# The last pooling layer multiplies before it takes its means, and state updates keep their traced place

## The chip, the cores and the metric

The kernel runs on one core of a Trainium2 chip. The metric is the device time of one execution in microseconds (us). The names are those of the profile: PE is the matrix engine (TensorE) and PEld its weight loads, DVE is VectorE, ACT is ScalarE, POOL is GpSimd, SP is the queue that issues most of the DMAs.

## The reference

One inference step of a four-layer decoder: 256 new prompt tokens and 8 sample tokens of width 1024, 264 columns in all. Each layer has a token mixer (pooling, gated delta rule, retention, pooling again) and then a dense feed-forward block (FFN), and each sublayer ends in a LayerNorm. Cut to what matters here:

```python
def pool_mixer(x, buf, n_valid, w, scale):            # four channel groups, windows 2, 4, 8, 16
    ext = concatenate([buf, x], axis=1)               # buf: the last 15 rows of the state
    c = pad(cumsum(ext, axis=1))
    for gi, win in enumerate(POOL_WINDOWS):
        s = c[:, P+1:P+1+T, lo:hi] - c[:, P+1-win:P+1-win+T, lo:hi]
        means.append(s / minimum(t + 1 + n_valid, win))
    pooled = concatenate(means, -1) - x
    return einsum('btgc,gcd->btgd', pooled, w) * scale, ext[:, -P:]

S = S * gl_n[..., None, None] + einsum('bhcd,bhce->bhde', kg_n, v_new)   # delta rule and retention alike

x = layer_norm(DN_ALPHA * x + mix, ln_g[i, 0], ln_b[i, 0])
x = layer_norm(DN_ALPHA * x + swiglu(x, ffn_w13[i], ffn_w2[i]), ln_g[i, 1], ln_b[i, 1])
```

The mean over tokens and the product with `w` over channels act on different axes, so either can come first.

## The kernel before

The activations lie transposed: 8 blocks of 128 channels, each 264 tokens wide. Every float32 operand is split into a rounded high part and a low rest, and `mm3` (L123 holds its matmuls) makes each product of three matmuls: high times high, low times high, high times low. Weights come in chunks of 1 MB into three `raw` buffers by SP; ACT casts the high part (L205), DVE takes the low part (L206), in `split`.

A norm can be **deferred** (class `LN`): the centred sum `d` times its gain goes into `zh` and `zl`, the next layer multiplies these at once, and only then do `stats` (L344) give the scale `r` and the shift `mr`. `unfold` (L397) repairs a product: one DVE instruction from the PSUM bank times `r`, one POOL addition. `apply` (L387) makes `x` itself: one DVE instruction, one POOL addition, and the split of `x` into `xh` and `xl`. A norm that is not deferred waits for `stats`, and `finish` (L376) makes `x`. Deferred are all norms but those after FFN 2 and FFN 3.

Each **FFN** (`ffn`, L444) has three stages on PE. In the first, steps j = 0 to 7 multiply `zh` and `zl`, and each step unfolds two products, gates them (`evac`) and applies one block of `x` (the *z stage* below). Steps 8 to 21 multiply `xh` and `xl` (the *x stage*). Then `w2` multiplies the gated `gh` and `gl` (the *g stage*). FFN 1 follows the delta rule and FFN 2 the retention layer; each also updates the 8 sample tokens' states of all 8 heads, in `gdn_states` (L413) and `ret_states` (L428). The program asks for four updates after every step from j = 8 on and after every second chunk of the g stage (`next(more, None)`), which ends in the g stage. An update is a multiplication on ACT (L421, L437) and one on DVE (L422, L438); a head's state and its new row come through two buffers each (SP loads `st` and `vbc`), and POOL stores the state.

A planner orders the instructions of every engine ahead of the run, by an estimate of when each is ready. Updates depend on little, so they can be placed far ahead of where the program asks for them. `tc.keep_in_program_order` ties an instruction behind the one that was traced before it on its engine; what is traced later can still pass it.

The **last pooling layer** (`pool_layer`, L497) follows FFN 2, whose norm is not deferred. It takes the window sums of `x` (L551, for window 16 on POOL), splits the means into `ph` and `pl` (L558, L559), multiplies them with its matrix, adds `ALPHA * x` (L568), and its own deferred norm makes `zh` and `zl` for FFN 3. Matmuls on a tile of ones (`busy`) fill PE's time meanwhile. The tile `d` has one buffer (L279), `zh` and `zl` share two (L286, L287).

Of the kernel before, what the change touches and what calls it, by code (L numbers as in the profile page):

```python
# [11 lines left out]
F32 = mybir.dt.float32  # L12
F32R = mybir.dt.float32r
# [98 lines left out]
def body(ctx: ExitStack, tc: tile.TileContext, ap):  # L112
# [75 lines left out]
    def nm(s):  # L188
        uid[0] += 1
        return f"{s}_{uid[0]}"  # L190

    def mm_ps(spare=False):
        if spare:
            return sm_ps([P, T + 2])
        return pmm.tile([P, T + 2], F32, tag="mm", name=nm("mm"))

    def sm_ps(shape):
        return psm.tile(shape, F32, tag="sm", name=nm("sm"))
# [70 lines left out]
    class LN:  # L269
# [3 lines left out]

        def __init__(self, idx, defer, on_pe=False):
            self.idx, self.defer, self.on_pe = idx, defer, on_pe
            self.c, self.seen = None, []
            self.d = pers.tile([P, KB, T], F32, tag="d", name=nm("d"))  # L279
            if on_pe:  # L280
                self.p1, self.p2 = sm_ps([P, T]), sm_ps([P, T])
            else:
                self.s1 = lnp.tile([P, T], F32, tag="s1", name=nm("s1"))
                self.s2 = lnp.tile([P, T], F32, tag="s2", name=nm("s2"))
            if defer:
                self.zh = pers.tile([P, KB, T + 2], F32R, tag="xz", name=nm("zh"), bufs=2)  # L286
                self.zl = pers.tile([P, KB, T + 2], F32R, tag="xz", name=nm("zl"), bufs=2)  # L287
                G.tensor_copy(self.zh[:, :, T:T + 2], gbh[:, idx])
                G.tensor_copy(self.zl[:, :, T:T + 2], gbl[:, idx])

# [93 lines left out]
                V.scalar_tensor_tensor(y, self.d[:, m], gm, self.r, MUL, MUL)  # L384
                S.activation(x[:, m], y, AF.Identity, bias=bm)  # L385

        def apply(self, m):  # L387

            u = lnp.tile([P, T], F32, tag="u", name=nm("u"), bufs=2)
            S.activation(u, self.mr, AF.Identity, scale=self.ng[:, m:m + 1], bias=W("lnb", self.idx * 8 + m))  # L390
            y = lnp.tile([P, T], F32, tag="y", name=nm("y"), bufs=2)
            V.scalar_tensor_tensor(y, self.d[:, m], self.g(m), self.r, MUL, MUL)
            G.tensor_tensor(x[:, m], y, u, ADD)
            S.copy(xh[:, m], x[:, m])  # L394
            V.tensor_tensor(xl[:, m], x[:, m], xh[:, m].bitcast(F32), SUB)  # L395

# [9 lines left out]
    def resid(ln, m, ps):  # L406
# [3 lines left out]
            V.tensor_tensor(ln.d[:, m], ps, ln.d[:, m], ADD)  # L410
        ln.block(m)

    def gdn_states(fp):  # L413

        for h in range(H):
            st = fp.tile([P, NB, P], F32, tag="st", name=nm("st"), bufs=2)
            vbc = fp.tile([P, NB, P], F32, tag="vbc", name=nm("vbc"), bufs=2)
            nc.sync.dma_start(st, ap["gst"][h])
            nc.sync.dma_start(vbc, vdg[h].rearrange("b e -> (b e)").partition_broadcast(P).rearrange("p (b e) -> p b e", b=NB))
            for b in range(NB):  # L420
                S.mul(st[:, b], st[:, b], egs[:, b, h:h + 1])  # L421
                V.scalar_tensor_tensor(st[:, b], vbc[:, b], ksg[:, h, b:b + 1], st[:, b], MUL, ADD)  # L422
                if b % 4 == 3:
                    if b > 4:
                        nc.gpsimd.dma_start(ap["gdn_s"][h], st)
                    yield

    def ret_states(fp):  # L428

        for h in range(H):  # L430
            st = fp.tile([P, NB, 256], F32, tag="st", name=nm("st"), bufs=2)
            vbc = fp.tile([P, NB, 256], F32, tag="vbc", name=nm("vbc"), bufs=2)
            nc.sync.dma_start(st, ap["rst"][h])
            nc.sync.dma_start(vbc, vdr[h].rearrange("b e -> (b e)").partition_broadcast(P).rearrange("p (b e) -> p b e", b=NB))
            for b in range(NB):
                if b % 2 == 0:
                    S.mul(st[:, b:b + 2], st[:, b:b + 2], 1.0 - 2.0 ** (-5.0 - h))  # L437
                V.scalar_tensor_tensor(st[:, b], vbc[:, b], ksr[:, h, b:b + 1], st[:, b], MUL, ADD)  # L438
                if b % 4 == 3:
                    if b > 4:  # L440
                        nc.gpsimd.dma_start(ap["ret_s"][h], st)
                    yield

    def ffn(l, pln):  # L444
        with tc.tile_pool(name=f"ffn{l}", bufs=1) as fp:
            gh = fp.tile([P, FB, T], F32R, name=nm("gh"))
            gl = fp.tile([P, FB, T], F32R, name=nm("gl"))

            more = (gdn_states if l == 1 else ret_states)(fp) if l in (1, 2) else iter(())

            def evac(j, pa, pb):
                s = fp.tile([P, T], F32, tag="s", name=nm("s"), bufs=2)
                S.activation(s, pa, AF.Silu)
                V.tensor_tensor(s, s, pb, MUL)
                S.copy(gh[:, j], s)
                V.tensor_tensor(gl[:, j], s, gh[:, j].bitcast(F32), SUB)

            for j in range(FB):
                if j < ND:
                    pss = proj2(ap["w13"][l, j], pln.zh, pln.zl, j == 2)  # L460
                    if j == 0:
                        pln.stats()
                    ab = [fp.tile([P, T], F32, tag="ab", name=nm("ab"), bufs=4) for _ in range(2)]
                    for e in range(2):
                        pln.unfold(pss[e], ab[e])
                    evac(j, *ab)
                    for m in range(KB * j // ND, KB * (j + 1) // ND):
                        pln.apply(m)
                else:
                    pa, pb = proj2(ap["w13"][l, j], xh, xl)  # L470
                    evac(j, pa[:, 0:T], pb[:, 0:T])
                    next(more, None)
            ln = LN(l * 2 + 1, l in (0, 1))
            tc.keep_in_program_order(S.preload_act_table_set("natural_log_exp_and_others"))
            hl = None
            ps = None
            for t in range(KB * FB):
                m, k = divmod(t, FB)
                if t % 16 == 0:
                    hl = chunk(ap["w2"][l, t // 16])  # L480
                if k == 0:
                    ps = mm_ps()
                mm3(ps[:, 0:T], hl[(t % 16) // 8], (t % 8) * 128, 128, gh[:, k], gl[:, k], k == 0, k == FB - 1)
                if k == FB - 1:
                    resid(ln, m, ps[:, 0:T])
                if t % 16 == 8:
                    next(more, None)
            assert next(more, None) is None
            if not ln.defer:
                ln.stats()  # L490
                for m in range(KB):
                    ln.finish(m)
                    if l == DEPTH - 1 and m % 2:
                        nc.sync.dma_start(ap["y"][:, m - 1:m + 1], x[:, m - 1:m + 1])
            return ln

    def pool_layer(l, j, _):  # L497
        with tc.tile_pool(name=f"pool{l}", bufs=1) as pp:
            st = pp.tile([P, KB, NB, 15], F32, name=nm("st"))
            ob = pp.tile([P, 512], BF16, name=nm("ob"))  # L500
# [900 lines left out]
```

## Time and profile before

| | us |
|---|---|
| median of 3 runs (lowest, highest) | 1423.22 (1420.69, 1425.02) |
| the profiled execution's own time | 1423.15 |
| its span, first to last instruction | 1421.4 |
| PE, DVE, ACT, POOL busy | 1335.9, 1043.1, 847.0, 458.4 |

Busy times are means over stages with different limits. The way to read this profile is to cut the span at the points where PE goes over from one kind of operand to the next (the first matmul on `zh`, on `xh`, on `gh`), and to compare like stages of the four FFNs, which do the same products.

### The profile page before, as it was taken

The numbers are of one execution on the slowest core, as the hardware profiler recorded it, in microseconds if no ns is written. First come the engines' busy times: TensorE is split into PE (matmuls) and PEld (weight loads), VectorE is DVE, ScalarE is ACT, GpSimd is POOL, SyncE is SP. The second block draws the span as 40 slices with busy tenths as digits, with TensorE's granted clock in tenths as the row PEclk, the third lists the DMA queues.
The fourth block names the chain that finished last, engine by engine and source line by source line (L and its number), as shares of the span: only waits on it lengthen the run. The fifth ranks groups of instructions, "written<-read, shape, count | busy, mean of one in ns | idle before, by whom it ended". The sixth has DMA issues, their size and how long they took to land. (4 is left out here: it accounts for less than half of the span.)

```text
span 1421.4 us, 27703 instructions
## 1 busy us (share of the span) xinstructions
PE 1335.9 (94%) x10506; PEld 1280.3 (90%) x10509; DVE 1043.1 (73%) x2075; ACT 847.0 (60%) x1975; POOL 458.4 (32%) x518
## 2 busy tenths in 40 slices
PE   7999999879999988999979999999899998999996
PEld 4999999768998987999979999998899995999996
DVE  8885566998666898656687867669987648885564
ACT  4674544759555688544476655547866444774543
POOL 5230013554352434001267755132400135330022
PEclk8999999899999999999999999999999998999998
DMA  6355555412222578555544644359798452355551
GB/s 226 119 181 179 178 179 199 148 60 90 90 96 79 206 285 280 178 179 177 195 179 153 224 171 177 140 178 362 280 394 311 176 180 89 119 189 181 179 183 42
DMA packets 44341, 257.06 MB, mean 181 GB/s; under 512 B 5040, under 2 KB 9776, under 8 KB 16560
## 3 DMA queue, kind: packets, MB, share of 16 engines
q1 hardware_dynamic: 35936, 223.17, 44.2%
q10 hardware_dynamic: 5968, 19.55, 3.8%
q0 software_dynamic: 2304, 12.58, 2.2%
q8 instruction: 82, 1.34, 0.4%
q14 instruction: 51, 0.42, 0.1%
HBM read 238.45 MB, written 16.84 MB: 180 GB/s over the span
## 5 line engine op out<-in xcount | busy, mean ns | idle before, releaser
L206 DVE TENSOR_TENSOR l<-raw,h 128x512 fp32r<-128x512 f32 x658 | 461.6, 737 | 149.9 <-ACT h L205 144.5
L205 ACT CAST h<-raw 128x512 fp32r<-128x512 f32 x680 | 386.9, 617 | 226.7 <-PE mm L123 180.1
L123 PE MATMUL mm<-xh,h 128*128 128x264 f32 x1216 | 346.5, 288 | 8.8 <-ACT xh L394 5.2
L123 PE MATMUL mm<-xl,h 128*128 128x264 f32 x1216 | 348.4, 288 | 6.0 <-DVE xl L395 6.0
L123 PE MATMUL mm<-xh,l 128*128 128x264 f32 x1216 | 343.8, 287 | 0.4 <-DVE l L206 0.4
L123 PEld LDWEIGHTS mm<-xh,h 128*128 128x128 f32 x1216 | 229.9, 190 | 11.4 <-ACT xh L394 6.3
L123 PEld LDWEIGHTS mm<-xl,h 128*128 128x128 f32 x1216 | 231.0, 190 | 7.0 <-DVE xl L395 6.6
L123 PEld LDWEIGHTS mm<-xh,l 128*128 128x128 f32 x1216 | 229.0, 190 | 1.0 <-DVE l L206 0.6
L123 PE MATMUL mm<-gh,l 128*128 128x264 f32 x704 | 200.7, 285 | 0.0
L123 PE MATMUL mm<-gh,h 128*128 128x264 f32 x704 | 200.3, 285 | 0.0
L123 PE MATMUL mm<-gl,h 128*128 128x264 f32 x704 | 198.7, 282 | 0.0
L123 PE MATMUL mm<-zh,h 128*128 128x266 f32 x496 | 144.7, 296 | 9.1 <-DVE ab L403 8.5
L123 PE MATMUL mm<-zh,l 128*128 128x266 f32 x496 | 143.3, 294 | 6.2 <-DVE l L206 6.2
L123 PE MATMUL mm<-zl,h 128*128 128x266 f32 x496 | 145.1, 294 | 0.0
L123 PEld LDWEIGHTS mm<-gh,h 128*128 128x128 f32 x704 | 132.5, 188 | 0.1
L123 PEld LDWEIGHTS mm<-gh,l 128*128 128x128 f32 x704 | 132.5, 188 | 0.1
L123 PEld LDWEIGHTS mm<-gl,h 128*128 128x128 f32 x704 | 132.6, 188 | 0.0
L313 POOL TENSOR_TENSOR s<-d 128x264 f32<-128x264 f32 x6 | 5.7, 942 | 361.7 <-DVE d L297 361.7
L123 PE MATMUL mm<-xh,w 128*128 128x264 f32 x416 | 108.8, 316 | 2.1 <-DVE ab L403 2.1
L123 PEld LDWEIGHTS mm<-zh,h 128*128 128x128 f32 x496 | 95.7, 194 | 11.2 <-ACT h L205 5.3
L123 PEld LDWEIGHTS mm<-zh,l 128*128 128x128 f32 x496 | 95.5, 194 | 8.1 <-DVE l L206 7.7
L404 POOL TENSOR_TENSOR ab<-ab,u 128x264 f32<-128x264 f32 x68 | 64.9, 963 | 116.3 <-PE mm L123 39.3
(403 smaller groups left out, 2792.8 us busy)
## 6 DMA issues: line engine op xcount, KB each, us to landing
raw<-in_w_dram SPq DMA_DIRECT2D x132, 1024.0 KB
raw<-in_rwi_dram SPq DMA_DIRECT2D x24, 1024.0 KB
raw<-in_gwi_dram SPq DMA_DIRECT2D x16, 1024.0 KB
st<-in_rst_dram ACTq DMA_DIRECT2D x8, 1024.0 KB
raw<-in_rwo_dram SPq DMA_DIRECT2D x8, 1024.0 KB
st<-in_rst_dram SPq DMA_DIRECT2D x8, 1024.0 KB
vbc<-vdr SPq DMA_DIRECT2D x8, 1024.0 KB
out_ret_s_dram<-st POOLq DMA_DIRECT2D x8, 1024.0 KB, 10.5
```

What stands on the lines that cost most here:

```text
L123: i = nc.tensor.matmul(*a, **k)
L205: S.copy(hi[:, w], src_ap[:, w])
L206: (E or V).tensor_tensor(lo[:, w], src_ap[:, w], hi[:, w].bitcast(F32), SUB)
L313: G.tensor_tensor(self.s1, d[:, self.seen[0]], d[:, m], ADD)
L404: (E or G).tensor_tensor(out, out, u[:n], ADD)
```

## The change

Two things are changed. First, each of the four kinds of state-update instruction is tied behind the instruction traced before it on its engine. Second, the norm after FFN 2 is deferred, and the last pooling layer is a new function: `pool_rows` (called at the start of FFN 2's g stage) loads the state rows and sums them into eight more columns of `zh` and `zl`; `pool_late` multiplies `zh`, `zl` with the matrix, takes `stats`, unfolds the products, and takes the window sums of these. `x` is made by `apply` without its split. The state of the last pooling layer is stored by POOL from a `raw` buffer.

```diff
-        return pmm.tile([P, T + 2], F32, tag="mm", name=nm("mm"))
+        return pmm.tile([P, n], F32, tag="mm", name=nm("mm"))
...
-                self.zh = pers.tile([P, KB, T + 2], F32R, tag="xz", name=nm("zh"), bufs=2)
-                self.zl = pers.tile([P, KB, T + 2], F32R, tag="xz", name=nm("zl"), bufs=2)
+                self.zh = pers.tile([P, KB, T + 2 + more], F32R, tag="xz", name=nm("zh"), bufs=2)
+                self.zl = pers.tile([P, KB, T + 2 + more], F32R, tag="xz", name=nm("zl"), bufs=2)
...
             G.tensor_tensor(x[:, m], y, u, ADD)
+            if not parts:
+                return
...
+    def later(i):
+        return tc.keep_in_program_order(i)
...
-                S.mul(st[:, b], st[:, b], egs[:, b, h:h + 1])
-                V.scalar_tensor_tensor(st[:, b], vbc[:, b], ksg[:, h, b:b + 1], st[:, b], MUL, ADD)
+                later(S.mul(st[:, b], st[:, b], egs[:, b, h:h + 1]))
+                later(V.scalar_tensor_tensor(st[:, b], vbc[:, b], ksg[:, h, b:b + 1], st[:, b], MUL, ADD))
...
-                    S.mul(st[:, b:b + 2], st[:, b:b + 2], 1.0 - 2.0 ** (-5.0 - h))
-                V.scalar_tensor_tensor(st[:, b], vbc[:, b], ksr[:, h, b:b + 1], st[:, b], MUL, ADD)
+                    later(S.mul(st[:, b:b + 2], st[:, b:b + 2], 1.0 - 2.0 ** (-5.0 - h)))
+                later(V.scalar_tensor_tensor(st[:, b], vbc[:, b], ksr[:, h, b:b + 1], st[:, b], MUL, ADD))
...
-            ln = LN(l * 2 + 1, l in (0, 1))
+            ln = LN(l * 2 + 1, l < DEPTH - 1, more=NB if l == 2 else 0)
+            if l == 2:
+                pool_rows(ln)
...
+    def pool_rows(ln):
+
+        st = wp.tile([P, CW], F32, tag="raw", name=nm("raw"))[:, 0:KB * NB * 15].rearrange("p (k b r) -> p k b r", k=KB, b=NB)
+        nc.sync.dma_start(st, ap["pst"][1])
+        nc.gpsimd.dma_start(ap["pool_o"][1], st)
+        ss = lnp.tile([P, KB, NB], F32, tag="ss", name=nm("ss"))
+        for g in range(4):
+            w = slice(2 * g, 2 * g + 2)
+            V.tensor_reduce(ss[:, w], st[:, w, :, 16 - (2 << g):15], AX.X, ADD)
+        zh, zl = (z[:, :, T + 2:T + 2 + NB] for z in (ln.zh, ln.zl))
+        S.copy(zh, ss)
+        V.tensor_tensor(zl, ss, zh.bitcast(F32), SUB)
+
+    def pool_late(l, j, pln):
...
+            raw = wp.tile([P, CW], F32, tag="raw", name=nm("raw"))
+            nc.sync.dma_start(raw, ap["pw"][j])
+            hl = [split(raw[:, i * 1024:(i + 1) * 1024], 1024, wp, "w", G) for i in range(2)]
...
+            def product(g):
+                for e in range(2):
+                    ps = pss[2 * g + e] = mm_ps(n=T + 2 + NB)
+                    for kk in range(2):
+                        mm3(ps, hl[g // 2], (g % 2) * 512 + kk * 256 + e * 128, 128, pln.zh[:, 2 * g + kk], pln.zl[:, 2 * g + kk], kk == 0, kk == 1)
+
+            product(0)
+            product(1)
+            pln.stats()
+            ln = LN(l * 2, True, True)
+            pob = sm_ps([P, 512])
+            busy(8)
+            for g in range(4):
+                b0 = 2 * g
+                win = 2 << g
+                E = G if g == 3 else V
+                y = pp.tile([P, 2, T], F32, tag="y", name=nm("y"), bufs=2)
+                rows = []
+                for e in range(2):
+                    ps = pss[b0 + e]
+                    pln.unfold(ps, y[:, e])
+                    rows.append(ps[:, T + 2:T + 2 + NB])
+                dst = pp.tile([P, 2, T], F32, tag="s0", name=nm("sw"), bufs=2)
+                if g == 0:
...
+                else:
+                    src = y
+                    for i in range(g + 1):
+                        sh = 1 << i
+                        if i:
+                            dst = pp.tile([P, 2, T], F32, tag=f"s{i % 2}", name=nm("sw"), bufs=2)
+                        E.tensor_tensor(dst[:, :, sh:TP], src[:, :, sh:TP], src[:, :, 0:TP - sh], ADD)
+                        S.copy(dst[:, :, 0:sh], src[:, :, 0:sh])
+                        src = dst
+                    for e in range(2):
+                        V.tensor_tensor(dst[:, e, TP:T], rows[e], y[:, e, TP:T], ADD)
+                    V.tensor_tensor(dst[:, :, 0:16], dst[:, :, 0:16], co[:, b0:b0 + 2], MUL)
+                    V.scalar_tensor_tensor(dst, dst, 1.0 / win, y, MUL, SUB)
+                if g < 2:
+                    product(g + 2)
+                for m in (b0, b0 + 1):
+                    pln.apply(m, False)
+                S.mul(ax[:, b0:b0 + 2], x[:, b0:b0 + 2], ALPHA)
+                if g:
+                    G.tensor_tensor(ax[:, b0:b0 + 2], ax[:, b0:b0 + 2], ln.c.unsqueeze(1).to_broadcast([P, 2, T]), SUB)
+                for e in range(2):
+                    m = b0 + e
+                    V.scalar_tensor_tensor(ln.d[:, m], dst[:, e], W("psc", j * 8 + m) if g else hps[:, e:e + 1], ax[:, m], MUL, ADD)
+                    if g:
+                        ln.centre(m, False)
+                if g == 0:
+                    ln.estimate(b0, b0 + 1)
+                if g < 3:
+                    busy(8)
...
```

## Rows read from the trace of the kernel before

**Rows 1.** The page's first part: busy us, share of the span, instructions

```profile
PE 1335.9 (94%) x10506; PEld 1280.3 (90%) x10509; DVE 1043.1 (73%) x2075; ACT 847.0 (60%) x1975; POOL 458.4 (32%) x518
```

**Rows 2.** Instructions on zh: count, ns min/median/max, first to last start, FFN 3

```profile
L123 PE MATMUL mm<-zh,h x112: 280/286/482, 1207.5 to 1257.9; 128*128 128x266 f32 x112
```

**Rows 3.** Busy time by stage: z of FFN 0, then z and x of FFN 1, 2, 3

```profile
core 0: us, PE busy (x) PEld busy (x) DVE busy (x) ACT busy (x) POOL busy (x), PEclk, DMA share, GB/s
35.70:87.00 51.30, 51.18 (x405) 50.59 (x404) 43.33 (x79) 37.34 (x91) 16.93 (x19) 1.00 0.38 127
...
486.90:549.70 62.80, 54.18 (x390) 51.50 (x389) 60.02 (x135) 51.33 (x139) 26.55 (x31) 0.95 0.80 288
549.70:641.40 91.70, 86.41 (x673) 84.99 (x674) 58.01 (x113) 52.93 (x119) 8.41 (x11) 0.96 0.57 194
963.00:1023.70 60.70, 52.91 (x390) 51.56 (x389) 57.33 (x114) 48.85 (x113) 18.78 (x23) 0.94 0.86 328
1023.70:1106.80 83.10, 82.67 (x675) 82.34 (x674) 65.62 (x128) 53.98 (x111) 10.00 (x12) 1.00 0.89 343
1207.50:1258.30 50.80, 50.80 (x405) 50.32 (x404) 43.64 (x79) 37.55 (x91) 17.26 (x19) 1.00 0.37 128
1258.30:1342.30 84.00, 82.99 (x674) 82.44 (x674) 52.17 (x94) 44.86 (x97) 5.12 (x6) 1.00 0.53 187
```

**Rows 4.** The state updates: count, ns min/median/max, first to last start

```profile
L421 ACT ACTIVATE st<-st,egs x64: 384/387/417, 490.9 to 564.7; 128x128 f32<-128x128 f32 x64
L422 DVE SCALAR_TENSOR_TENSOR st<-vbc,ksg,st x64: 338/341/849, 497.0 to 565.1; 128x128 f32<-128x128 f32 x64
L437 ACT ACTIVATE st<-st x32: 612/620/635, 968.1 to 1090.0; 128x512 f32<-128x512 f32 x32
L438 DVE SCALAR_TENSOR_TENSOR st<-vbc,ksr,st x64: 472/480/980, 971.8 to 1092.2; 128x256 f32<-128x256 f32 x64
```

**Rows 5.** Retention states: waits at FFN 2's start, stores to landing, a stretch's DMA rate

```profile
968.14 2.19 ACT L437 ACTIVATE st<-st 128x512 f32<-128x512 f32 x4 [0.91 <-DMA st<-in_rst_dram]
...
971.79 1.67 DVE L438 SCALAR_TENSOR_TENSOR st<-vbc,ksr,st 128x256 f32<-128x256 f32 x4 [2.72 <-DMA vbc<-vdr]
...
out_ret_s_dram<-st POOLq DMA_DIRECT2D x8, 1024.0 KB, 10.5
...
1035.00:1040.00 5.00, 5.00 (x44) 5.00 (x43) 4.42 (x9) 3.77 (x10) 0.00 (x0) 1.00 1.01 426
```

**Rows 6.** DVE and ACT in order of time around the last pooling layer: start, us

```profile
1171.41 0.43 DVE L410 TENSOR_TENSOR d<-mm,d 128x264 f32<-128x264 f32 x1 [6.56 <-PE mm L123]
...
1179.04 0.43 DVE L368 SCALAR_TENSOR_TENSOR r<-t,r 128x264 f32<-128x264 f32 x1
...
1205.82 0.64 ACT L558 ACTIVATE ph<-sw 128x528 fp32r<-128x528 f32 x1 [1.02 <-DVE sw L557]
...
1210.14 1.11 DVE L568 SCALAR_TENSOR_TENSOR d<-mm,vec,ax 128x264 f32<-128x264 f32 x2 [2.95 <-PE mm L123]
```

**Rows 7.** Busy time by stage, columns as above: from the norm's r to FFN 3

```profile
1179.50:1207.50 28.00, 22.94 (x97) 15.38 (x97) 25.43 (x40) 15.80 (x40) 14.18 (x13) 0.82 0.13 43
```

**Rows 8.** DVE and POOL in order of time, alone and beside each other

```profile
525.59 0.42 DVE L403 TENSOR_TENSOR ab<-mm,r 128x264 f32<-128x264 f32 x1
...
1182.79 0.48 DVE L384 SCALAR_TENSOR_TENSOR y<-d,vec,r 128x264 f32<-128x264 f32 x1
...
1188.95 0.69 DVE L557 SCALAR_TENSOR_TENSOR sw<-sw,x 128x528 f32<-128x528 f32 x1
...
1191.56 1.80 DVE L557 SCALAR_TENSOR_TENSOR sw<-sw,x 128x528 f32<-128x528 f32 x1
...
1189.71 4.81 POOL L562 TENSOR_TENSOR ax<-ax,c 128x528 f32<-128x528 f32 x3 [1.72 <-ACT c L331]
```

**Rows 9.** The additions of unfold and apply on POOL: count, ns min/median/max

```profile
L404 POOL TENSOR_TENSOR ab<-ab,u x68: 743/938/1966, 50.8 to 1264.2; 128x264 f32<-128x264 f32 x68
...
L393 POOL TENSOR_TENSOR x<-y,u x48: 736/768/1622, 54.6 to 1265.4; 128x264 f32<-128x264 f32 x48
```

## What I expect and why

> **What bounds the kernel now.** I read the page's busy shares first: PE is busy 94% of the span, DVE 73% [rows 1]. That says PE's stream is the bound on the whole, but not where it stands still. So I cut the span where PE's operands change (FFN 3's first `zh` is one such cut [rows 2]) and compared like stages [rows 3]. An undisturbed z stage takes 51.3 us (FFN 0) or 50.8 us (FFN 3), an x stage 84.0 us (FFN 3). FFN 1 takes 62.8 and 91.7 us for the same products, FFN 2 60.7 and 83.1 us. The excess over FFN 3 is 12.0 + 7.7 = 19.7 us in FFN 1 and 9.9 - 0.9 = 9.0 us in FFN 2. DVE says why: it is busy 60.0 of 62.8 us and 57.3 of 60.7 us in the two slow z stages, against 43.6 of 50.8 us in FFN 3's [rows 3]. What is extra there are the state updates. The program asks for them from step 8 on, but they start at 490.9 us in FFN 1 and 968.1 us in FFN 2, the z stages' first microseconds, and the 64 of FFN 1 are over by 565 us [rows 4]. So in two z stages DVE and ACT are the bound, not PE. The third place is the gap around the last pooling layer: FFN 2's last product reaches DVE at 1171.41 us, the norm's `r` is done at 1179.47 us, and FFN 3's first matmul is at 1207.5 us [rows 2, 6]. In those 28.0 us after `r` DVE is busy 25.4 us [rows 7].
>
> **The updates, FFN 1.** Tied behind the gating of step 8, 9, ..., none can run in the z stage any more. The z stage then holds what FFN 0's and FFN 3's hold: 62.8 to 51 us, -11.8. The x stage loses its backlog: 91.7 to 84.0, -7.7. Against this, 14 of the 16 groups of four go into the x stage: 56 x 0.338 = 18.9 us of DVE on 52.2 of 84.0, so 71, and 56 x 0.387 = 21.7 us of ACT on 44.9, so 67 [rows 3, 4]. FFN 2's x stage shows DVE at 65.6 of 83.1 without loss [rows 3]; 71 is a little past what is shown, and I charge 1.5 us. The other 8 updates lie in the g stage beside matmuls that leave both engines room; if that cover were gone they would cost 8 x 0.34 = 2.7 us. **Sum: -18** (from -19.7 to -13, where each of the six heads loaded late holds ACT for 1 us).
>
> **The updates, FFN 2.** z stage 60.7 to 51: -9.7. The x stage has its share already (it is at 83.1) and gets more: 56 x 0.48 = 26.9 us of DVE on 52.2, so 79 of 84, and 28 x 0.62 = 17.4 of ACT [rows 3, 4]. Two costs have no row of their own. One is DVE at 94%. The other is the transfer: a head needs 1 MB in, 1 MB of its broadcast row and 1 MB out per two steps, beside 2 MB of weights, so some 5.2 MB in 12 us, 437 GB/s, where the busiest stretch that I found moved 426 [rows 5]. With two buffers a head's load waits for the store two heads back: 8 us of updates, 10.5 us of store [rows 5] and a load of 5 to 9 us (the first landings, by 968.1 and 971.8, against the stage's start at 963.0 [rows 3, 5]) are 24 to 28 us, where program order leaves 24. Nothing below zero can come of either. Above, I take 3.5 us, between 0 (the present x stage: its DMA share is 0.89 and PE loses nothing [rows 3]) and 10 (six late heads, each losing about what the first wait of ACT and half of DVE's show [rows 5]). **Sum: -6** (-9.7 to 0).
>
> **The last pooling layer.** Before `r`: the deferred norm adds a subtraction and two sums on DVE for the last block and 24 matmuls of the first two products (24 x 0.125 us, as in FFN 3's x stage with 674 in 84.0 us [rows 3], 3 us of PE) ahead of the norm's own; it removes the subtraction of the mean on seven blocks on POOL. I hold `r` at 8 us after the last product, within 1 us either way. The deferred work of the other blocks (a subtraction and a split each, 0.43 and 0.48 us by like instructions [rows 6, 8]) lies in FFN 2's g stage beside matmuls; uncovered it would be 8 x 0.9 = 7 us. The state rows' load and store move there too, and take one of three weight buffers for some 10 us; a chunk lasts PE 48 x 0.125 = 6.0 us, so two buffers still cover; if not, one late chunk costs up to 5 us. SP gets one load more, and POOL's queue a store behind the last state's.
>
> After `r`: removed are the split of the means (4 x 0.69 us on DVE, by the like instruction of that width [rows 8]) and, for the last window, the way from the means (ACT at 1205.82) over the split and PE to `d` (1210.14), 4.3 us [rows 6], and PE's last 12 products (1.5 us). Added on DVE are 8 products by `r` (0.42 each, from PSUM), one more product for three blocks of `x` (0.48) and one for `mr`: 3.4 + 1.4 + 0.4 - 2.8 = +2.4 us [rows 8]. Added on POOL are 16 additions of 0.74 us at the least for three products gone: 13 x 0.74 = +9.6 us [rows 9], on 14.2 us of 28 [rows 7]. If both engines ran freely beside each other, POOL would be busy 24 of 28 us, DVE 28, and the 4.3 + 1.5 us would be gained: **-6** is the low end. But the rows show them in each other's way: the same DVE instruction takes 0.69 us alone and 1.80 us while POOL subtracts [rows 8]. If all of it adds up, and the 8 instructions that make `d` (0.48 us), which now read two SBUF operands, too, it is 2.4 + 9.6 + 3.9 - 1.5 = **+14**. DVE and POOL together were busy 39.6 us in those 28 [rows 7], so about a third overlaps even with the waits counted in; half of 12 us hidden, less the 1.5 us of matmuls, is **+4**, which I take. Two more orderings point the same way: the new `d` shares its one buffer with the old, so no `d` is written before all eight `apply` have read, and the new `zh` waits for the last product.
>
> The Trainium skill, "SBUF — State Buffer", section "Who interferes with whom", says that a DVE instruction with two SBUF inputs and a GpSimd instruction that reads SBUF block each other for the whole instruction. The trace agrees in kind: 1.80 against 0.69 us [rows 8]. Taken to the letter it gives the +14 above.
>
> **Sum.** The profiled execution took 1423.15 us, 0.07 from the median of the runs, so no correction: 1423.15 - 18 - 6 + 4 = **1403 us**.
>
> **Rivals.** (1) The pooling gap shrinks as POOL and DVE overlap: -6 instead of +4, **1393 us**. For it: POOL was busy only 14.2 of 28 us [rows 7]. Against: the 1.80 us. (2) DVE and POOL exclude each other wholly: +14, **1413 us**. For it: [rows 8]; against: a third did overlap. (3) Slower: the tied multiplication stands in ACT's queue until its state has landed, and behind it stand the casts of the next weights, for which PE waits. The trace has this wait: 0.91 us on ACT, 2.72 us on DVE for the row [rows 5]. Twelve heads are loaded while their predecessors are stored; if each costs PE over 20 / 12 = 1.7 us the gain is gone, and at 2.7 us each, 32 us, it is **1435 us**. Against: in FFN 2's x stage, with DMA at 0.89, PE lost nothing. (4) The tie doesn't do what it says, as later work passes it or the z stages are bound by something else; then only the pooling gap counts: 1423 + 4 = **1427 us**.
>
> **How the numbers follow.** Forecast (1397 to 1409) 0.50; rival 1 0.17; rival 2 0.15; rival 3 0.11; rival 4 0.07. Beyond 0.3% (4.3 us), about what a measurement of this kernel can tell from no change, faster are the forecast and rivals 1 and 2, 0.82; rival 4, at +0.27%, is within: 0.07; rival 3 is slower: 0.11. The range leaves out rivals 3 and 4 and reaches past rivals 1 and 2 by the bounds of the updates' terms: 1387 to 1418.
>
> **What would show it.** Updates that first start behind the first `xh` matmul in both FFNs; z stages of about 51 us with DVE near 43; x stages of 85 us in FFN 1 and 86 to 87 in FFN 2; 32 us from `r` to FFN 3's first `zh` with POOL busy over 22. Wrong would be: z stages still near 60 (rival 4), waits of ACT for `st` with PE idle behind (rival 3), or a gap clearly under 28 or over 40 us.

## The result and the profile after

| kernel | median us (lowest, highest) | ratio to before, 95% interval |
|---|---|---|
| before | 1422.53 (1420.69, 1425.02) | |
| after | 1411.97 (1409.22, 1414.71) | 0.9925 [0.9897, 0.9952] |

The change saves 10.6 us, 0.75%. The forecast was 20 us. The profiled execution of the changed kernel took 1410.32 us and its span is 1408.2 us, 13.2 less than before.

The page's first part, after (busy us, share of the span, instructions; before: [rows 1]):

```profile
PE 1324.0 (94%) x10477; PEld 1272.9 (90%) x10481; DVE 1051.9 (75%) x2099; ACT 853.6 (61%) x1996; POOL 466.3 (33%) x528
```

Busy time by stage, after, columns as in [rows 3]: z and x of FFN 1, z, x and g of FFN 2, then from FFN 2's last matmul to FFN 3's first `xh`, and FFN 3's x stage.

```profile
488.00:540.60 52.60, 50.78 (x390) 48.88 (x389) 51.34 (x90) 38.75 (x93) 23.10 (x25) 1.00 0.54 183
540.60:624.60 84.00, 83.01 (x674) 82.44 (x673) 65.66 (x146) 60.09 (x149) 9.99 (x15) 1.00 0.81 287
943.30:994.00 50.70, 49.56 (x391) 48.55 (x390) 46.37 (x84) 37.85 (x92) 17.80 (x19) 1.00 0.60 232
994.00:1084.20 90.20, 84.08 (x675) 82.57 (x673) 66.16 (x137) 57.21 (x119) 9.64 (x15) 1.00 0.88 335
1084.20:1150.70 66.50, 66.29 (x529) 66.01 (x530) 49.50 (x90) 38.01 (x74) 16.68 (x19) 0.97 0.76 286
...
1150.70:1246.80 96.10, 76.04 (x505) 67.78 (x506) 79.20 (x144) 66.71 (x158) 48.08 (x51) 0.88 0.28 97
...
1246.80:1329.30 82.50, 82.50 (x674) 82.26 (x673) 51.28 (x92) 43.72 (x95) 3.67 (x5) 1.00 0.51 183
```

FFN 2's z stage and FFN 1's x stage are at the undisturbed lengths of [rows 3], FFN 1's z stage within 1.8 us of them. FFN 2's x stage is not: 90.2 us with PE busy 84.1, so PE stands still for 6.1 us, where it stood still for 0.4 before. The line 1150.70:1246.80 is the last pooling layer with FFN 3's z stage; PE is busy 76 of 96 us in it and DVE 79. The updates now start behind the first `xh` matmul of their FFN (540.6 and 994.0 us), as the tie demands (count, ns min/median/max, first to last start; before: [rows 4]):

```profile
L426 ACT ACTIVATE st<-st,egs x64: 386/389/403, 553.3 to 632.8; 128x128 f32<-128x128 f32 x64
...
L443 DVE SCALAR_TENSOR_TENSOR st<-vbc,ksr,st x64: 472/476/982, 1007.7 to 1125.2; 128x256 f32<-128x256 f32 x64
```

Cut at the same points, the stages of the main kernels compare as follows (us, one profiled execution each; "gap" is from FFN 2's last matmul on `gh` or `gl` to FFN 3's first on `xh`, and so holds FFN 3's z stage). The last four columns are experiments told below.

| stage | before | after | ties alone | layer alone | `ret_spread` | `ret_three` |
|---|---|---|---|---|---|---|
| FFN 1 z | 62.8 | 52.6 | 52.6 | 62.9 | 52.6 | 52.6 |
| FFN 1 x | 91.7 | 84.0 | 84.0 | 91.1 | 84.0 | 84.0 |
| FFN 2 z | 60.7 | 50.7 | 50.7 | 60.8 | 50.7 | 50.7 |
| FFN 2 x | 83.1 | 90.2 | 87.9 | 82.9 | 83.9 | 84.8 |
| FFN 2 g | 64.3 | 66.5 | 65.4 | 64.3 | 64.9 | 66.6 |
| gap | 87.2 | 96.1 | 84.6 | 96.1 | 96.1 | 84.9 |
| FFN 3 x | 84.0 | 82.5 | 84.0 | 82.5 | 82.7 | 84.0 |

From before to after this is -17.9 in FFN 1, -10.0, +7.1 and +2.2 in FFN 2's three stages, +8.9 in the gap and -1.5 behind it, together -11.2; the other 2 us of the 13.2 lie in stretches that the change doesn't touch (+1.2 ahead of FFN 1, -3.0 in the retention layer, -0.2 at the end).

### The profile page after: what moved, and what is told of

Read it like the earlier page. It is cut to its first block, busy times and chain, and to the rows that moved or that the text cites. A ratio compares the mean times of both kernels' runs of the same rounds, so it can differ in the third digit from the quotient of the medians.

```text
span 1408.2 us, 27679 instructions
## 1 busy us (share of the span) xinstructions
PE 1324.0 (94%) x10477; PEld 1272.9 (90%) x10481; DVE 1051.9 (75%) x2099; ACT 853.6 (61%) x1996; POOL 466.3 (33%) x528
## 3 DMA queue, kind: packets, MB, share of 16 engines
q1 hardware_dynamic: 35648, 224.22, 44.6%
## 5 line engine op out<-in xcount | busy, mean ns | idle before, releaser
L123 PE MATMUL mm<-zh,h 128*128 128x266 f32 (+1 forms) x512 | 148.4, 294 | 8.5 <-DVE sw L562 6.6
L123 PE MATMUL mm<-zh,l 128*128 128x266 f32 (+1 forms) x512 | 147.0, 291 | 2.5 <-DVE l L206 2.4
L123 PE MATMUL mm<-zl,h 128*128 128x266 f32 (+1 forms) x512 | 148.6, 292 | 0.0
L406 POOL TENSOR_TENSOR ab<-ab,u 128x264 f32<-128x264 f32 x68 | 68.3, 1016 | 136.2 <-DVE ab L405 58.9
L123 PEld LDWEIGHTS mm<-zl,h 128*128 128x128 f32 x512 | 97.9, 191 | 1.2 <-DVE zl L300 0.2
## 6 DMA issues: line engine op xcount, KB each, us to landing
out_ret_s_dram<-st POOLq DMA_DIRECT2D x8, 1024.0 KB, 10.2
```

Source lines behind the costliest of these rows:

```text
L123: i = nc.tensor.matmul(*a, **k)
L406: (E or G).tensor_tensor(out, out, u[:n], ADD)
```

## The experiments

Each kernel was run in several rounds beside the kernel before (medians 1421.8 to 1423.9 us there).

**The two parts, each alone.** `pins_only` is the kernel before with the four ties, `pool_only` the changed kernel without them.

```diff
-                S.mul(st[:, b], st[:, b], egs[:, b, h:h + 1])
+                later(S.mul(st[:, b], st[:, b], egs[:, b, h:h + 1]))
...
```

> The kernel before with the state updates tied and the old pooling layer. Theory A: the ties gain 18 us in FFN 1, 3 in the retention layer and 10 in FFN 2's z stage, and cost FFN 2's x stage 1 us or less; the loss of 7 us there after the change came from the state rows of the pooling layer, which held a weight buffer. Then the time is 1391 to 1395 us, the x stage of FFN 2 at 83 to 85 us, the gap and FFN 3's z stage as before (36 and 51 us). Theory B: the tied updates themselves cost FFN 2 its 9 us, as ACT waits for states or the transfers are full: 1399 to 1403 us with an x stage of 88 us or more.

> The changed kernel with the updates free as before: the new pooling layer alone. Theory A: the new layer costs 9 us from FFN 2's last product to FFN 3's first xh product, and the state rows that take a weight buffer cost FFN 2 up to 4 us more: 1431 to 1436 us. Theory B: the layer costs 9 us only there, FFN 2 takes what it took before: 1430 to 1432 us. Were the layer a gain by itself, it would be under 1420 us.

Measured: the ties alone 1397.74 us (1394.92 to 1398.98), 0.9831 [0.9814, 0.9847]; the layer alone 1429.38 us (1428.84 to 1431.22), 1.0053 [1.0038, 1.0068]. The first lies between its two theories, the second is 0.6 us under theory B. The ties gain 25 us and the layer loses 7. Together they would give -18 and give -10.6, so there is a loss that only the pair has. The table shows 6 us of it: FFN 2's x and g stages are 2.3 and 1.1 us longer in after than with the ties alone, and the gap is 11.5 us longer where the layer alone costs it 8.9, because the ties with the old layer had shortened it by 2.6 (why, no run here settles).

**FFN 2's x stage: engines or transfers?** `few_rows` loads the broadcast rows of two heads only, `slow_ret` asks for updates at every second x step; both are the kernel before with the ties.

```diff
+            if h < 2:
+                vbcs.append(fp.tile([P, NB, 256], F32, tag="vbc", name=nm("vbc"), bufs=2))
+            vbc = vbcs[h % 2]
...
+            if h < 2:
+                nc.sync.dma_start(vbc, vdr[h].rearrange("b e -> (b e)").partition_broadcast(P).rearrange("p (b e) -> p b e", b=NB))
```

> Ties alone with the old pooling layer, and the new rows of the retention states loaded for the first two heads only; the other six use these, which leaves out 6 MB of the 24 MB that the states move and nothing of the engines' work. Theory A (transfers): x stage of FFN 2 from 87.9 to 84 or 85 us, time 1392 to 1395 us. Theory B (engines): x stage stays at 87 to 88, time 1396 to 1399 us.

```diff
-                    next(more, None)
+                    if l != 2 or j % 2 == 0:
+                        next(more, None)
```

> Ties alone with the old pooling layer, and the retention states asked for after every second step of FFN 2's x stage, so that more of them fall into its g stage. With the ties alone FFN 2's x stage took 87.9 us and its g stage 65.4. Theory A (the states' transfers and waits at one head per two steps are what slows it): x stage 84 to 85, g stage 64.3 to 65, time 1392 to 1394 us. Theory B (DVE's share of the work is what slows it, wherever it lies): no gain, 1396 to 1399 us.

Measured: `few_rows` 1391.9 us (1391.62 to 1392.62), 0.9782 [0.9766, 0.9798]; `slow_ret` 1401.67 us (1401.43 to 1403.07), 0.9852 [0.9837, 0.9866]. FFN 2's x stage, first with the ties alone, then with fewer rows (columns as in [rows 3]):

```profile
992.20:1080.10 87.90, 84.40 (x674) 82.74 (x673) 66.69 (x134) 55.38 (x117) 9.16 (x14) 1.00 0.88 334
```

```profile
993.70:1077.60 83.90, 82.89 (x675) 82.42 (x674) 69.54 (x141) 57.39 (x121) 9.64 (x15) 1.00 0.85 317
```

With 6 MB less to move, DVE and ACT do more in the stage (69.5 and 57.4 us against 66.7 and 55.4), and the stage is 4 us shorter, at the undisturbed 84. So the engines had room, and the 4 us come with the row loads. Whether it is their bytes is not shown, since `few_rows` also takes their place out of SP's queue, where weight loads stand behind them. With the ties alone SP waited there for a free row buffer (SP's waits in this stage: us in total, times, longest), and with fewer rows it had no such wait:

```profile
SPq L437 <- DVE st L441: 20.1, 3, 9.0
```

ACT's wait for a state, the mechanism of the slower rival, is in the trace but not six times (waits of the ties alone in this stage: us in total, times, longest):

```profile
ACT st L440 <- DMA st<-in_rst_dram: 4.5, 2, 3.2
```

`slow_ret` mends the stage too (83.9 us), as its theory A had it, and yet is 4 us slower than the ties alone, which neither theory had. Its gap grew by 10.5 us, and the next experiment shows how.

**Where may the updates go instead?** `ret_spread` asks at every second x step and then at every twelfth product of the g stage; `ret_three` at 11 of the 14 x steps and at every eighth product.

```diff
+                    if l != 2 or j % 2 == 0:
...
-                if t % 16 == 8:
+                if t % (12 if l == 2 else 16) == (0 if l == 2 else 8):
```

> The kernel before with the tied updates, where FFN 2's x stage asks for retention updates only at every second of its 14 steps and its g stage at every twelfth of 176 products instead of every sixteenth, so that the last of the 17 requests falls about 40 us into the g stage and not at its end. Theory (the transfers of the states need room beside the weights, and the pooling layer's start needs them landed by the end of FFN 2): x stage of FFN 2 83.9 us as with every second step alone, g stage 64.3 to 65, from its end to FFN 3's first xh product 84 to 86 us as with the ties alone, and so 4 to 5 us less than the ties alone: median 1392 to 1394 us. Rival (stretching the updates into the g stage itself delays the pooling layer, whatever the time at which they end there): x stage 83.9 us, but 90 to 95 us from FFN 2's end to the first xh product, median 1399 to 1404 us.

```diff
+                    if l != 2 or j % 4 != 3:
...
-                if t % 16 == 8:
+                if t % (8 if l == 2 else 16) == (0 if l == 2 else 8):
```

> The kernel before with the tied updates, where FFN 2's x stage asks for retention updates at 11 of its 14 steps and its g stage at every eighth product from the first on: the last of the 17 requests falls at the 41st of 176 products, as with the ties alone. Theory (the x stage's 4 us are lost to state transfers beside the weights, and the start of the pooling layer needs only that the last state is stored well before FFN 2 ends): 3 requests or some 4.5 MB leave the x stage, which takes 84 to 86 us instead of 87.9; last store landed before 1140 us, from FFN 2's end to the first xh product 84 to 86 us as with the ties alone; median 1394 to 1396.5 us against 1397.7. Rival (any shift of the requests moves the last state's load and with it the last updates past the end of FFN 2, as with every second step): x stage 84 to 86 us but 93 to 96 us to the first xh product, median 1400 to 1404 us.

Measured: `ret_spread` 1401.79 us (1400.82 to 1403.39), 0.9852 [0.9836, 0.9868]; `ret_three` **1394.45 us** (1393.26 to 1396.14), 0.9807 [0.9786, 0.9827]. In the first the expectation failed though the x stage was mended: the gap is 96.1 us, with the old pooling layer. DVE in order of time at FFN 2's end (start, us; FFN 2's last product starts at 1143.7):

```profile
1144.40 3.25 DVE L441 SCALAR_TENSOR_TENSOR st<-vbc,ksr,st 128x256 f32<-128x256 f32 x8
...
1158.13 0.48 DVE L505 MEMSET ob<- 128x512 bf16 x1 [0.27 <-DMA out_ret_s_dram<-st]
1158.53 0.63 DVE L546 TENSOR_TENSOR sw<-x 128x510 f32<-128x510 f32 x1
```

and POOL:

```profile
1147.35 6.50 POOL L360 TENSOR_TENSOR d<-d,mr 128x264 f32<-128x264 f32 x6 [2.83 <-ACT mr L355]
1153.80 0.57 POOL L444 DMA_DIRECT2D out_ret_s_dram<-st  x1
```

The last head's eight updates stand behind FFN 2's end, although the program asks for them at the 97th of its 176 products: the load of its state was issued at 1122.77, where the ties alone issue it at 1104.54 and do the updates at 1122.3. They are done at 1147.65, but the store stands behind POOL's six subtractions of the mean and is issued at 1153.80. The pooling layer's tiles lie in FFN 2's space, so their first writer, the `memset` of `ob`, waits until that store has landed. The filling matmuls read `ob`, and PE runs 43 of them before the layer's first product, whose operand `pl` DVE had ready at 1164.0:

```profile
1159.26 10.88 PE L123 MATMUL sm<-ob 128*128 128x512 bf16 x43 [12.52 <-DVE sw L546]
1169.80 0.47 PE L123 MATMUL mm<-ph,h 128*128 128x264 f32 x1
```

So `c`, which the norm's later blocks need, comes 34.9 us after FFN 2's end instead of 18.0. The updates may move, then, only if the last store leaves well before FFN 2 ends. `ret_three` does that (stores issued, POOL):

```profile
1108.74 0.57 POOL L444 DMA_DIRECT2D out_ret_s_dram<-st  x1 [3.60 <-ACT h L205]
1118.70 0.57 POOL L444 DMA_DIRECT2D out_ret_s_dram<-st  x1 [3.61 <-ACT h L205]
```

Its x stage is 84.8, its gap 84.9 us, near the 84.6 of the ties alone, all as its theory had it; its g stage takes back 1.2 us. It is the fastest whole kernel here, 1.9% under before and 1.2% under after; against the ties alone its interval overlaps a little.

**The rows buffer.** In after, the state rows of the pooling layer come into one of the three weight buffers. `own_rows` gives them a tile of their own.

```diff
-        st = wp.tile([P, CW], F32, tag="raw", name=nm("raw"))[:, 0:KB * NB * 15].rearrange("p (k b r) -> p k b r", k=KB, b=NB)
+        st = fp.tile([P, KB, NB, 15], F32, name="prows")
```

> The changed kernel with the state rows of the last pooling layer in a tile of their own in place of a weight buffer. Theory A: FFN 2's weights have three buffers again, its x stage falls from 90 to 84 us, its g stage from 67 to 65, and the time to 1402 to 1405 us. Theory B (the tied updates are what slows FFN 2): no change, 1409 to 1414 us.

Measured: 1406.8 us (1405.38 to 1409.95), 0.9895 [0.9877, 0.9912], FFN 2's x stage 88.7 us for 90.2. After's SP queue in that stage (start, us):

```profile
1058.64 0.33 SPq L211 DMA_DIRECT2D raw<-in_w_dram  x1
1061.45 0.33 SPq L507 DMA_DIRECT2D raw<-in_pst_dram  x1
1067.94 0.33 SPq L439 DMA_DIRECT2D vbc<-vdr  x1
1069.14 0.33 SPq L211 DMA_DIRECT2D raw<-in_w_dram  x1
...
1078.14 0.33 SPq L211 DMA_DIRECT2D raw<-in_w_dram  x1
```

The program asks for these rows at the start of the g stage; the planner put the load 23 us earlier, into the x stage. POOL issues the store at 1069.4 and it lands 11.4 us later, so one buffer is away for 19 us, and with two left the weight loads around it are issued 10.5 and 9.0 us apart, where PE uses a chunk in 6. PE pays right there (stretches of 5 us, after):

```profile
1075.00:1080.00 5.00, 5.00 (x39) 4.81 (x40) 3.59 (x10) 3.30 (x6) 0.00 (x0) 1.00 1.02 429
1080.00:1085.00 5.00, 1.92 (x14) 1.48 (x12) 1.69 (x4) 3.47 (x6) 0.00 (x0) 1.00 1.01 423
1085.00:1090.00 5.00, 5.00 (x29) 5.00 (x30) 5.00 (x12) 4.76 (x10) 0.00 (x0) 0.66 0.83 297
```

PE stands still for 3 us with DMA at full share, and in the next 5 us the granted clock is 0.66 on average, between its levels of 1.2 and 2.4 GHz. Not all of the 3 us need be the buffer's: ACT, which casts that chunk, also loads a table there (L458, 1.28 us from 1081.03). With a tile of their own for the rows the same 5 us are whole:

```profile
1080.00:1085.00 5.00, 5.00 (x43) 5.00 (x42) 5.00 (x13) 3.71 (x8) 0.53 (x1) 1.00 0.99 403
```

The own tile wins back 1.5 of the 2.3 us by which after's x stage is longer than with the ties alone; the medians moved by 5, with intervals that overlap. Neither theory gave these numbers: the x stage stays over 84 us because most of its excess is there with the ties alone. After's g stage (66.5 us) doesn't get shorter by it (66.7), so the rows buffer is not its cause, and that 1.1 us stays open.

**The pooling layer: three suspects.** Each was taken out of after alone: the additions on POOL (`adds_on_dve`), the one buffer of `d` (`own_d`), the filling matmuls between the groups (`no_busy`).

```diff
-            G.tensor_tensor(x[:, m], y, u, ADD)
+            (G if parts else V).tensor_tensor(x[:, m], y, u, ADD)
...
-                    pln.unfold(ps, y[:, e])
+                    pln.unfold(ps, y[:, e], E=V)
```

> The changed kernel with the 16 additions of unfold and apply in the last pooling layer on DVE instead of POOL. Theory A: DVE and POOL stand in each other's way there, so 16 x 0.43 = 6.9 us more on DVE cost less than 16 additions of 0.74 to 1.0 us on POOL did: the time from r to the last zl falls from 36 us to 30 to 33, and the whole to 1406 to 1409 us. Theory B: DVE alone is the bound and POOL is beside it: 7 us longer, 1417 to 1420 us. Theory C: neither, the order of PE's matmuls behind the last zl sets the end: within 2 us of 1412.

```diff
-            self.d = pers.tile([P, KB, T], F32, tag="d", name=nm("d"))
+            self.d = (dp or pers).tile([P, KB, T], F32, tag="d", name=nm("d"))
...
+        dp = ctx.enter_context(tc.tile_pool(name="late", bufs=1))
...
-            ln = LN(l * 2, True, True)
+            ln = LN(l * 2, True, True, dp=dp)
```

> The changed kernel with a tile of its own for d of the last pooling layer's norm, so that it can be written before every apply of the norm before has read the old d. In the changed kernel the first d comes 29.8 us after FFN 2's last product, the norm's c 32.5 us, the first xh product 96 us. Theory A (the shared buffer holds the chain back): first d at 17 to 21 us, c at 20 to 24, first xh product at 86 to 91, time 1402 to 1407 us. Theory B (DVE and POOL are full in that stretch whatever the order): c earlier, but the last zl stays at 44 to 47 us and the first xh product at 94 to 97, time 1409 to 1414 us.

```diff
-                if g < 3:
-                    busy(8)
```

> The changed kernel without the 24 matmuls on ones between the groups of the last pooling layer (the 8 ahead of the groups stay). In the changed kernel 21 of them run after the first zl, in PE's stream ahead of FFN 3's products. Theory A (PE's order behind the last zl sets the end): 24 x 0.216 = 5 us of PE go, the first xh product comes at 91 to 93 us instead of 96, time 1407 to 1409 us. Theory B: PE waits for zl anyway and the clock falls for want of work: 95 to 98 us, time 1411 to 1414 us.

| us after FFN 2's last matmul | `r` | first `d` | `c` | last `zl` | 48th z matmul of FFN 3 | first `xh` | median |
|---|---|---|---|---|---|---|---|
| before | 8.4 | 16.4 | 18.5 | 42.4 | 44.6 | 87.2 | 1422.5 |
| after | 9.9 | 29.8 | 32.5 | 46.1 | 54.1 | 96.1 | 1412.0 |
| `adds_on_dve` | 9.9 | 27.7 | 31.1 | 45.0 | 53.2 | 95.2 | 1408.9 [0.9888, 0.9919] |
| `own_d` | 9.9 | 16.6 | 18.7 | 48.6 | 47.8 | 95.9 | 1410.9 [0.9899, 0.9935] |
| `no_busy` | 9.9 | 29.9 | 32.5 | 46.1 | 48.5 | 92.7 | 1408.6 [0.9881, 0.9920] |

None of the three is the cause by itself, and each one's interval overlaps with after's. With its own `d` the layer makes `c` 14 us earlier and wins nothing, since the last `zl` comes 2.5 us later (theory B, but for this `zl`). Without the filling matmuls PE catches up sooner behind the last `zl`, and the first `xh` comes 3.4 us earlier, as theory A of `no_busy` had it. The additions are the surprise. DVE's groups from `r` to the last `zl` (group x count, busy us, mean ns, idle time), after:

```profile
L392 DVE SCALAR_TENSOR_TENSOR y<-d,vec,r 128x264 f32<-128x264 f32 x8 | 6.0, 776 | 0.6 <-POOL x L393 0.6
...
L571 DVE TENSOR_TENSOR sw<-y 128x510 f32<-128x510 f32 x2 | 2.0, 987 | 0.0
```

and with the additions on DVE:

```profile
L392 DVE SCALAR_TENSOR_TENSOR y<-d,vec,r 128x264 f32<-128x264 f32 x8 | 3.7, 487 | 0.0
...
L406 DVE TENSOR_TENSOR y<-y,u 128x264 f32<-128x264 f32 x8 | 3.3, 427 | 0.0
L393 DVE TENSOR_TENSOR x<-y,u 128x264 f32<-128x264 f32 x8 | 3.3, 426 | 0.0
...
L571 DVE TENSOR_TENSOR sw<-y 128x510 f32<-128x510 f32 x2 | 1.4, 684 | 0.0
```

DVE takes 16 instructions more and is busy no longer (the stretch from `r` to the last `zl`, columns as in [rows 3]; after, then with the additions on DVE):

```profile
1160.60:1196.80 36.20, 19.79 (x81) 14.68 (x83) 33.45 (x58) 19.90 (x52) 26.25 (x28) 0.67 0.01 4
```

```profile
1161.90:1197.00 35.10, 19.82 (x79) 14.92 (x80) 32.86 (x73) 19.98 (x52) 12.16 (x12) 0.66 0.01 4
```

What POOL took off DVE, it took back by slowing DVE down: without the 6.6 us of additions DVE is busy 26.3 us, 7.2 less than in after, where the same additions took POOL 14.1 us. Theory A of `adds_on_dve` had this right, and the median is in its range, but the stretch falls by 1.1 us only, to 35.1 and not to 33. In either form DVE is busy over 92% of it.

**Where the layer's 8.9 us lie.** By the table, 1.5 us come before `r`, 2.2 between `r` and the last `zl`, and 5.2 behind the last `zl`. The last two stretches, before:

```profile
1179.50:1213.50 34.00, 28.94 (x144) 21.32 (x144) 28.57 (x46) 18.66 (x47) 14.18 (x13) 0.85 0.11 36
1213.50:1258.30 44.80, 44.80 (x357) 44.39 (x356) 40.50 (x73) 34.69 (x85) 17.26 (x19) 1.00 0.42 145
```

and the last one after:

```profile
1196.80:1246.80 50.00, 49.95 (x388) 48.66 (x387) 39.34 (x73) 39.59 (x92) 20.15 (x21) 1.00 0.40 142
```

Behind the last `zl` PE is busy all the time in both; after, it has 388 matmuls left there for 357. Between `r` and the last `zl` it stood still for 16.4 us, at a granted clock of 0.67 on average, where before the change it stood still for 5.1 us, at 0.85. Of the 5.2 us, `no_busy` gives back 3.4.

The 1.5 us before `r` have a cause that no run takes away. The old layer asks for ACT's table for `Ln` and `Exp` ahead of FFN 2's end (`preload_act_table_set`, L532 of the kernel before); `pool_late` doesn't, and ACT loads a table before each of the two. After, ACT and then DVE, which waits for it:

```profile
1155.75 1.28 ACT L364 ACT_TABLE_LOAD   x1
1157.05 0.42 ACT L364 ACTIVATE r<-vv 128x264 f32<-128x264 f32 x1
1157.49 1.28 ACT L365 ACT_TABLE_LOAD   x1
1158.78 0.42 ACT L365 ACTIVATE r<-r 128x264 f32<-128x264 f32 x1
...
1159.24 0.43 DVE L366 TENSOR_TENSOR t<-r 128x264 f32<-128x264 f32 x1 [2.92 <-ACT r L365]
```

Before, the same two instructions:

```profile
1176.36 0.42 ACT L364 ACTIVATE r<-vv 128x264 f32<-128x264 f32 x1 [2.94 <-DVE ss L554]
1176.81 0.42 ACT L365 ACTIVATE r<-r 128x264 f32<-128x264 f32 x1
```

`vv` is ready at 1156.32, so the two loads cost this chain 2.0 us. All forms of the new layer that were run have them, and two more in FFN 3's `stats`.

**All three at once, and then less work for DVE.** `late_mix` has the three edits together; `late_light` is `late_mix` without the additions of `u` in the layer's unfold and apply.

> The changed kernel with three of its traits taken away at once: the norm of the pooling layer has a buffer of its own for d, the sums of the unfold and of apply run on VectorE instead of GpSimd, and the filling matmuls between the groups are left out. Each alone brought 0 to 3.4 us. Theory (the three stand in for each other, so that only all together free the layer): last zl product operand at 40 to 43 us after FFN 2's end, first xh product at 85 to 88 us instead of 96.1, median 1400 to 1404 us. Rival (the work of VectorE and GpSimd between r and the last zl fills the stretch in any order; VectorE alone would have some 31 us of it by the times that its instructions take alone): last zl at 44 to 48 us, first xh product at 91 to 95 us, median 1406 to 1411 us.

```diff
+            if not parts:
+                V.scalar_tensor_tensor(x[:, m], self.d[:, m], self.g(m), self.r, MUL, MUL)
+                return
...
-            (E or G).tensor_tensor(out, out, u[:n], ADD)
+            if add:
+                (E or G).tensor_tensor(out, out, u[:n], ADD)
...
-                    pln.unfold(ps, y[:, e], E=V)
+                    pln.unfold(ps, y[:, e], add=False)
```

> The version of the changed kernel with a d of its own, the sums on VectorE and no filling matmuls, which had its last zl at 48.0 us after FFN 2's end and FFN 3's first xh product at 92.1 us, and a median of 1407.5 us. Here the additions of u that end the unfold and apply of the pooling layer are left out: 16 VectorE instructions, 7.4 us of the 36.1 that VectorE was busy in the 38.1 us from r to the last zl (part of the computation is not done, so the time stands for the cost of that work alone). Theory (VectorE has no idle time left there, and its work sets the end of the layer): last zl at 40 to 42 us, first xh product at 84 to 87 us, median 1399 to 1403 us. Rival (the round of PE, VectorE and ScalarE through the four groups sets the end, and VectorE is only kept filled): last zl at 46 us or later, first xh product at 90 us or later, median 1405 us or more.

Measured: `late_mix` 1407.49 us (1406.64 to 1408.36), 0.9892 [0.9874, 0.9909]; `late_light` 1402.33 us (1399.78 to 1407.37), 0.9863 [0.9837, 0.9889]. My theory for `late_mix` fell: last `zl` at 48.0, first `xh` at 92.1 us, as the rival had it. That of `late_light` held. From `r` to the last `zl`, `late_mix` and then `late_light`:

```profile
1159.60:1197.70 38.10, 26.89 (x140) 23.51 (x141) 36.05 (x77) 22.25 (x58) 15.51 (x12) 0.82 0.09 31
```

```profile
1160.90:1191.10 30.20, 23.14 (x113) 20.70 (x114) 29.24 (x59) 20.59 (x57) 11.61 (x12) 0.72 0.08 26
```

With 7.4 us of additions left out, the last `zl` comes 7.9 us earlier, at 40.1, and the first `xh` 6.4 us earlier, at 85.7. So in this form of the layer the amount of DVE's work sets its end. The old layer, with the ties alone, has 46 DVE instructions and 28.1 us in the like stretch of 32.3 us:

```profile
1153.00:1185.30 32.30, 26.21 (x149) 18.88 (x147) 28.12 (x46) 18.26 (x47) 16.22 (x14) 1.00 0.12 41
```

No form of the new layer that was run beats the old one. The table loads are a part of this that was not tested: in `late_mix` PE stands still once behind the last `zl`, for the unfolding that waits for FFN 3's `r` (us in total, times, longest):

```profile
PE mm L123 <- DVE ab L405: 3.6, 1, 3.6
```

By an estimate from the rows above, its first `xh` would come at 87.5 us at best without the loads (92.1, less 2.0 before `r` and two times 1.28 there), which is still behind the 84.6 of the ties alone.

## Why the direction was right and the size was not

**The bound and the ties: right.** The z stages were long because the updates lay in them, and the tie moved them out; the rival by which the tie does nothing is out.

**FFN 1, -18: measured -17.9.** z stage -10.2 for -11.8 (it came to 52.6, not 51), x stage -7.7 as forecast, and the 1.5 us charged for DVE at 71 us did not come: DVE had 65.7 us there and PE lost nothing.

**FFN 2, -6: measured -10.0 + 4.8 = -5.2 with the ties alone, +1.1 in the g stage.** z stage -9.7 forecast. The x stage's 3.5 us were right in size (4.8), and of the two unknown costs it was the transfer's, by its bytes or by SP's waits for row buffers, which no run tells apart: DVE came to 66.7 us, not 79, and to 69.5 without loss with fewer rows loaded. The slower rival's mechanism (ACT's queue held by a late state) was there with 4.5 us in two waits, far from the 2.7 us for each of twelve heads that it needed.

**What after lost beyond that: a step that failed.** I wrote that the state rows take one of three weight buffers "for some 10 us" in the g stage and that "two buffers still cover; if not, one late chunk costs up to 5 us". The load was moved into the x stage, where the transfers were full already, and the buffer was away for 19 us; after's x stage is 2.3 us longer than with the ties alone, of which a tile of its own gave back 1.5. I counted on the cover of the g stage, and the planner put the load where there was none.

**The last pooling layer, +4: measured +6.9** with the layer alone (its gap is 8.9 us longer, FFN 3's x stage 1.5 shorter), inside the bounds of -6 to +14. The times of both rivals on it, free overlap and full exclusion, are out. But the 8.9 us don't lie where the sum has them, so that it came near is luck in part.

- I held `r` at 8 us after the last product, within 1. It came at 9.9, 1.5 later than before. The term that I left out is ACT's table loads, 2.0 us on this chain; without them `r` would have come at 7.9.
- "Half of 12 us hidden" is near what the additions show: of 14.1 us on POOL, 7.2 came back as slower DVE instructions. But the way from `r` to the last `zl` grew by 2.2 us and not by 4.
- FFN 3's z stage behind it I put at nothing, and 5.2 us were lost behind the last `zl`. 3.4 of these are the filling matmuls in PE's order; the other 1.8 stay open.

The Trainium skill, "SBUF — State Buffer", section "Who interferes with whom", was the reason for the upper end. That a DVE instruction with two operands in SBUF fell from 776 to 487 ns when POOL's additions were gone agrees with it. The +14 added all of POOL's new work to DVE's, and that much was not paid. Of the two orderings that I let "point the same way", the shared `d` is real (`c` 14 us later) and cost nothing that DVE's work wouldn't cost anyway: with a `d` of its own nothing was won.

**The sign that I named was the wrong one.** I said that 32 us from `r` to FFN 3's first `zh` would show the loss, with POOL over 22. The first `zh` came 25.9 us after `r`, earlier than before [rows 7], with POOL at 22.0, and the z stage behind it took 60.3 us instead of 50.8 [rows 3] (after, columns as in [rows 3]):

```profile
1160.60:1186.50 25.90, 9.54 (x33) 7.07 (x33) 23.44 (x41) 15.60 (x41) 21.99 (x25) 0.58 0.01 4
...
1186.50:1246.80 60.30, 60.20 (x437) 56.27 (x437) 49.34 (x91) 43.89 (x105) 24.40 (x25) 0.98 0.34 118
```

An early first matmul is no gain when the last operand is late.

**The sum.** The profiled execution missed 1403 us by 7.3: 5.3 in FFN 2's stages (-0.7 for -6), 3.4 in the gap and the x stage behind it (+7.4 for +4), 0.1 in FFN 1, less 1.8 in the two stretches ahead of FFN 1 and of FFN 2, which the change doesn't touch; 0.3 are outside these cuts.

## What to carry to other kernels

Tying filler work to its place in the program can be worth more than the restructuring next to it: measure the parts of a change apart, because here one gained 25 us and the other gave back 14 of it. Filler that carries transfers had two limits here, the transfers beside the weights and the landing of its last store before the next stage takes over its memory, so it was better thinned out a little (11 of 14 steps) than by half. Moving work from DVE to POOL was no relief here, where both read SBUF: count DVE's own time in the stretch before and after. Look for what the old version did ahead of time, such as a table load, and whether the new one still does it. And judge a pipeline's start by its last operand, not by its first matmul.

## What the runs showed of the hardware

- 16 additions moved from POOL to DVE left DVE's busy time as it was (33.45 to 32.86 us) and cut POOL's by 14.1 us: the same DVE instruction took 776 ns on average beside POOL's additions and 487 ns without.
- POOL's store of a 1 MB state took 8.7 to 13.3 us to land in FFN 2's x stage with the ties alone, where DMA runs at full share for long stretches, and 4.4 us late in its g stage; behind FFN 2's end, in `ret_spread` and `slow_ret`, it took 4.1.
- A store's landing delays an instruction that has nothing to do with it but its memory: the `memset` of `ob` waited for the last state's store in `ret_spread` and in `slow_ret`, and the pooling layer's first product with it.
- A table load took ACT 1.28 us, one before `Ln` and one before `Exp`, where the kernel before, which asks for the table ahead, shows none between `vv` and `r`.
